# First feed-forward block as plain products, raw chunks of both weights in one tile, pools on 64 bytes

## The chip, the cores and the metric

The kernel runs on one core of one Trainium2 chip. The metric is device time in microseconds (us), the median of several runs of the whole program; lower is better. All times below are us, unless ns is written. PE is TensorE, DVE is VectorE, ACT is ScalarE, SP is SyncE, which issues the weight loads.

## The reference

One decoder layer on a residual stream x of 256 rows and 2,048 columns, in fp32: two half-weight SwiGLU feed-forwards around a mixer (gated linear attention beside block attention) and a cross-attention.

```python
D_MODEL = 2048; SEQ = 256; D_FF = 5632

def swiglu(h, w_gate, w_up, w_down):
    return (jax.nn.silu(h @ w_gate) * (h @ w_up)) @ w_down

x = x + 0.5 * swiglu(rms_norm(x, ffn1_norm[l]), ffn1_w_gate[l], ffn1_w_up[l], ffn1_w_down[l])
u = rms_norm(x, mix_norm[l]) @ w_in[l]      # split into the inputs of the two head groups
x = x + jnp.concatenate([o_gla, o_moba], axis=-1) @ w_out[l]
x = x + memory_cross_attn(rms_norm(x, xattn_norm[l]), rms_norm(mem, mem_norm[l]), ...)
x = x + 0.5 * swiglu(rms_norm(x, ffn2_norm[l]), ffn2_w_gate[l], ffn2_w_up[l], ffn2_w_down[l])
```

## The kernel before

**Products.** Each fp32 product is made of three products of rounded halves (`mm3`): high by high, high by low, low by high, 512 columns wide, into one PSUM bank. A weight comes raw from memory in chunks of 128 rows by 512 columns, two chunks in one load of 512 KB (`load_raw`, issued by SP, tag `raw`, five buffers). ACT writes its high half (`whi`, L142), DVE subtracts that from the raw one for the low half (`wlo`, L143); both tags have five buffers of two chunks (three in the mixer).

**Feed-forward (`ffn`).** The 5,632 hidden columns are 11 blocks of 512, in groups of 4, 4 and 3. For a block, `Pair` makes gate and up for both halves of the rows together, on seven of the eight PSUM banks, in eight steps of two chunks of 128 of the 2,048 input rows. In its first four steps (S) it forms sums of raw gate and up chunks (tag `st`, four DVE operations of 512, L217 to L220), splits four things (the gate's two chunks, the up's second chunk u1 as `hu`/`lu`, and the two tiles of sums) and makes seven threefold products, against rows of x and prepared sums of them (`eh`/`el`). The last four steps (N) split gate and up plainly and make eight threefold products, against x and its differences (`dh`/`dl`). That is 84 + 96 = 180 products for a pair; plain gate and up would take 192. `early`, `gates` and `ups` then combine the banks on DVE (seven operations of 512), and L422 multiplies gate and up. `turn` transposes the result for the down product while the next pair runs; `pump` puts such pieces of work behind each step. After a group, four down blocks use its 16 (or 12) chunks. `run_blocks(late=True)` leaves the last four chunks of the first two blocks for behind the remaining work of `turn` (`drain`).

**Norm (`Normed`).** x is normed in four blocks of 512 columns: PE transposes four tiles of 128 (L315) into the one auxiliary bank, DVE scales them (`xg`, L318, with a broadcast gain), ACT and DVE split them (`xhi`, `xlo`), and for the pairs the sums of x for S steps (L364, and `eh`/`el`) or its differences for N steps (L369, and `dh`/`dl`) follow. In both feed-forwards this goes on while the first pair's products run.

**Order.** Each engine runs its instructions in one order, set before the program runs by the framework's scheduler, which also takes the waits for buffers from the pools. So lines of code and places in an engine's order differ, as the listings below show.

## Time and profile before

| | |
|---|---|
| median of three runs | 2019.07 (2018.95 to 2019.37) |
| profiled execution | 2019.1, its span 2017.4 |
| mean granted PE clock | 0.994 of full |
| PE busy | 1966.3 (97%) |
| DVE busy | 1531.9 (76%) |
| ACT busy | 1061.7 (53%) |
| weights moved | 369 MB, 183 GB/s in the mean |
| first pair of feed-forward 1, of 2 | 13.8 to 81.6, 1273.6 to 1335.4 |

A busy time is the time in which an engine executes something. Of an average over a span that has stages with different limits one learns little; the rows below are therefore taken by stretch. A start-to-start time of two neighbours is what an operation costs a busy engine; the recorded duration of one is longer, since neighbours overlap. In a row with square brackets the engine was idle for the time in them, up to the operation named.

### The profile page before, as it was taken

The page shows a single profiled execution, that of the slowest core. Times are in us where ns is not written, and L with a number is a line of the kernel's source. Part 1 is how long each engine was busy: PE and PEld are TensorE (multiplying, and loading weights), DVE is VectorE, ACT ScalarE, POOL GpSimd, SP SyncE. Part 2 cuts the span into 40 slices and gives each one's busy share as a digit, 9 for nine tenths or more (in the row PEclk, how much of TensorE's full clock was granted, in tenths as well). Part 3 has the DMA queues.
Part 4 walks back from the last instruction along what each step waited for, and adds up shares of the span by engine and source line. Part 5 has one row for each costly group of instructions (what it writes and reads, how often), then busy time and mean ns, then how long its engine had stood idle before and what let it go on. Part 6 is the DMA issues. An engine that isn't in the chain of part 4 may idle for free.

```text
span 2017.4 us, 24213 instructions
## 1 busy us (share of the span) xinstructions
PE 1966.3 (97%) x8848; PEld 1588.0 (79%) x8848; DVE 1531.9 (76%) x1974; ACT 1061.7 (53%) x1326; POOL 23.5 (1%) x52
## 2 busy tenths in 40 slices
PE   6999999999999999999999999899999999999999
PEld 4777888778887788887788888677788777888777
DVE  7998569996599865455765767999856999569974
ACT  5655445564455545544564646655544565445542
POOL 0000000000000000010000000000000000000000
PEclk8999999999999999999999999899999999999999
DMA  4566665556665656565456545366655556655564
GB/s 157 187 191 207 200 190 173 187 188 219 194 193 187 198 161 187 154 201 159 142 168 204 171 158 186 95 197 210 196 189 170 186 191 199 213 188 188 177 220 136
DMA packets 195487, 369.19 MB, mean 183 GB/s; under 512 B 11716, under 2 KB 22168, under 8 KB 195368
## 3 DMA queue, kind: packets, MB, share of 16 engines
q1 hardware_dynamic: 195368, 367.65, 57.6%
q8 instruction: 69, 1.13, 0.2%
q14 instruction: 50, 0.41, 0.1%
HBM read 365.50 MB, written 2.10 MB: 182 GB/s over the span
## 4 chain that ended last, share of the span: by engine, by line
PE 77%; DVE 16%; ACT 2%; issue 2%; DMA 2%; ACTq 0%; SPq 0%; DVEq 0%
PE mm L154 25%; PE mm L155 25%; PE mm L156 24%; DVE wlo L143 7%; ACT whi L142 2%; DVE st L217 1%; DMA raw<-in_ffn_w_up_dram 1%; DVE st L218 1%; DVE t2k L422 1%; DVE st L219 1%; DVE st L220 1%; DVE lu L143 1%; PE aux L315 1%; DVE biglo L143 0%; DVE xlo L143 0%
## 5 line engine op out<-in xcount | busy, mean ns | idle before, releaser
L143 DVE TENSOR_TENSOR wlo<-raw,whi 128x1024 fp32r<-128x1024 f32 (+3 forms) x616 | 732.6, 1200 | 389.6 <-ACT whi L142 388.8
L142 ACT ACTIVATE whi<-raw 128x1024 fp32r<-128x1024 f32 (+3 forms) x616 | 630.0, 1037 | 616.9 <-PE mm L156 510.4
L155 PE MATMUL mm<-wlo,xhi 128*128 128x512 f32 (+2 forms) x1240 | 485.0, 391 | 3.7 <-DVE wlo L143 3.7
L154 PE MATMUL mm<-whi,xhi 128*128 128x512 f32 (+2 forms) x1240 | 482.7, 393 | 1.0 <-ACT whi L142 1.0
L156 PE MATMUL mm<-whi,xlo 128*128 128x512 f32 (+2 forms) x1240 | 480.2, 387 | 0.0
L156 PE MATMUL mm<-whi,biglo 128*128 128x512 f32 x864 | 338.5, 392 | 0.0
L154 PE MATMUL mm<-whi,bighi 128*128 128x512 f32 x832 | 329.9, 396 | 0.0
L155 PE MATMUL mm<-wlo,bighi 128*128 128x512 f32 x832 | 323.9, 389 | 0.0
L155 PEld LDWEIGHTS mm<-wlo,xhi 128*128 128x128 f32 x1240 | 234.4, 189 | 53.1 <-DVE wlo L143 10.5
L154 PEld LDWEIGHTS mm<-whi,xhi 128*128 128x128 f32 x1240 | 234.0, 189 | 48.8 <-ACT whi L142 2.1
L156 PEld LDWEIGHTS mm<-whi,xlo 128*128 128x128 f32 x1240 | 234.3, 189 | 47.1
L142 ACT ACTIVATE whi<-st 128x1024 fp32r<-128x1024 f32 x176 | 185.8, 1059 | 130.2 <-DVE st L218 59.2
L143 DVE TENSOR_TENSOR wlo<-st,whi 128x1024 fp32r<-128x1024 f32 x176 | 212.6, 1220 | 6.2 <-ACT whi L142 5.0
L156 PEld LDWEIGHTS mm<-whi,biglo 128*128 128x128 f32 x864 | 162.2, 188 | 37.6
L155 PEld LDWEIGHTS mm<-wlo,bighi 128*128 128x128 f32 x832 | 156.3, 188 | 33.3
L154 PEld LDWEIGHTS mm<-whi,bighi 128*128 128x128 f32 x832 | 156.5, 188 | 30.9
L154 PE MATMUL mm<-whi,eh 128*128 128x512 f32 x264 | 106.1, 417 | 18.9 <-ACT whi L142 16.5
L155 PE MATMUL mm<-wlo,eh 128*128 128x512 f32 x264 | 106.8, 405 | 2.5 <-DVE wlo L143 1.0
L156 PE MATMUL mm<-whi,el 128*128 128x512 f32 x264 | 103.4, 392 | 0.0
L142 ACT ACTIVATE hu<-raw 128x512 fp32r<-128x512 f32 x88 | 55.4, 630 | 87.7 <-DMA raw<-in_ffn_w_up_dram 59.7
L154 PEld LDWEIGHTS mm<-whi,eh 128*128 128x128 f32 x264 | 49.3, 193 | 45.1 <-ACT whi L142 36.6
L217 DVE TENSOR_TENSOR st<-raw,raw 128x512 f32<-128x512 f32 x88 | 60.6, 688 | 23.7 <-DMA raw<-in_ffn_w_up_dram 22.9
(211 smaller groups left out, 1833.6 us busy)
## 6 DMA issues: line engine op xcount, KB each, us to landing
raw<-in_ffn_w_gate_dram SPq DMA_DIRECT2D x176, 512.0 KB, 4.6
raw<-in_ffn_w_up_dram SPq DMA_DIRECT2D x176, 512.0 KB, 3.9
raw<-in_ffn_w_down_dram SPq DMA_DIRECT2D x176, 512.0 KB, 4.1
raw<-in_w_in_dram SPq DMA_DIRECT2D x80, 512.0 KB, 3.9
raw<-in_w_out_dram SPq DMA_DIRECT2D x32, 512.0 KB, 3.6
raw<-in_w_in_dram SPq DMA_DIRECT2D x16, 344.0 KB, 3.1
raw<-in_xattn_w_kv_dram SPq DMA_DIRECT2D x8, 512.0 KB, 3.6
raw<-in_xattn_w_q_dram SPq DMA_DIRECT2D x8, 512.0 KB, 3.5
```

Of the source, the lines that this page charges most:

```text
L142: nc.scalar.activation(hi, src, AF.Copy)
L143: nc.vector.tensor_tensor(lo, src, hi.bitcast(F32), op=ALU.subtract)
L154: nc.tensor.matmul(p, a[0], w[0], start=start, stop=False)
L155: nc.tensor.matmul(p, a[0], w[1], start=False, stop=False)
L156: nc.tensor.matmul(p, a[1], w[0], start=False, stop=stop)
L217: nc.vector.tensor_tensor(sa[:, 0, :], g[:, 0, :], u[:, 0, :], op=ALU.add)
L218: nc.vector.tensor_tensor(sa[:, 1, :], u[:, 0, :], u[:, 1, :], op=ALU.add)
L219: nc.vector.tensor_tensor(sb[:, 0, :], sa[:, 0, :], u[:, 1, :], op=ALU.add)
L220: nc.vector.tensor_tensor(sb[:, 1, :], sb[:, 0, :], g[:, 1, :], op=ALU.add)
L315: nc.tensor.transpose(pt[:, i, :], c[:, i * P:(i + 1) * P], ident)
L422: nc.vector.scalar_tensor_tensor(u, u, r, g, op0=ALU.mult, op1=ALU.mult)
```

## The change

The lines of the kernel after are other ones: the sums are at L232, L234 and L235, `split_to` at L153 (DVE), the products at L165 to L167, the transposes of the norm at L328, the scaling at L331.

- The first block of each feed-forward is a plain gate block and a plain up block, two banks each, through `run_blocks(late=True)`. `gate_done` takes silu from PSUM on ACT, `up_done` multiplies on DVE. The other ten blocks stay pairs.
- A raw tile holds four chunks; there are three. A plain block loads four chunks in one DMA (1 MB). A pair's step loads gate into slots 1 and 2 and up into slots 0 and 3 of one tile, so the two sums (gate's first + up's first, up's first + up's second) are one DVE operation of 1,024 with a broadcast operand.
- `whi` and `wlo` have six buffers, and u1 takes one of these; `hu` and `lu` go.
- Ahead of the norm only the first four gate chunks are loaded.
- The two tiles of gains get a size that is a multiple of 64 bytes, by which all pools behind them start at such a multiple (before: 32 bytes off). In the mixer two small constants share the tile of `mqT`, which is made later.

```diff
@@ -43,8 +43,8 @@
 OFF_MQ = OFF_LR + RANK
 OFF_MK = OFF_MQ + BH * DH
 OFF_MV = OFF_MK + BH * DH
-RAWS = 5
-HIS = 5
+RAWS = 3
+HIS = 6
 T2K = 7
 KINDS = "SSSSNNNN"
 
@@ -94,8 +94,8 @@
     nc.scalar.activation(warm, warm, AF.Silu)
     ident = const.tile([P, P], F32, name="ident")
     make_identity(nc, ident)
-    gT1 = const.tile([P, KC], F32, name="gT1")
-    gT2 = const.tile([P, 4 * KC + 4], F32, name="gT2")
+    gT1 = const.tile([P, 32], F32, name="gT1")[:, :KC]
+    gT2 = const.tile([P, 96], F32, name="gT2")[:, :4 * KC + 4]
     gT = [gT1] + [gT2[:, i * KC:(i + 1) * KC] for i in range(4)]
     g_mq, g_mk, g_xq, g_xk = (gT2[:, 4 * KC + i:4 * KC + i + 1] for i in range(4))
 
@@ -128,26 +128,37 @@
 
     ahead = {}
 
-    def load_raw(k0, c0, w, n=NB):
-
-        raw = wp.tile([P, 2, n], F32, tag="raw", name=nm("raw"))
-        nc.sync.dma_start(raw, w[k0 * P:(k0 + 2) * P, c0:c0 + n].rearrange("(k p) n -> p k n", p=P))
+    def raw_tile():
+        return wp.tile([P, 4, NB], F32, tag="raw", name=nm("raw"))
+
+    def load_raw(k0, c0, w, n=NB, step=4):
+
+        raw = raw_tile()[:, :step, :n]
+        nc.sync.dma_start(raw, w[k0 * P:(k0 + step) * P, c0:c0 + n].rearrange("(k p) n -> p k n", p=P))
         return raw
 
-    def take_raw(k0, c0, w, n=NB):
+    def take_raw(k0, c0, w, n=NB, step=4):
         key = id(w), k0, c0
-        return ahead.pop(key) if key in ahead else load_raw(k0, c0, w, n)
+        return ahead.pop(key) if key in ahead else load_raw(k0, c0, w, n, step)
+
+    def load_pair(k0, c0, wg, wu):
+
+        raw = raw_tile()
+        for dst, w in ((raw[:, 1:3, :], wg), (raw[:, 0:4:3, :], wu)):
+            nc.sync.dma_start(dst, w[k0 * P:(k0 + 2) * P, c0:c0 + NB].rearrange("(k p) n -> p k n", p=P))
+        return raw
 
     def split_to(hi, lo, src):
         nc.scalar.activation(hi, src, AF.Copy)
         nc.vector.tensor_tensor(lo, src, hi.bitcast(F32), op=ALU.subtract)
 
-    def split_raw(raw, n=NB):
-
+    def split_raw(raw):
+
+        k, n = raw.shape[1:]
         bufs = 3 if "mix" in pools else HIS
-        hi, lo = (tmp_tile([P, 2, n], tag, bufs, F32R) for tag in ("whi", "wlo"))
+        hi, lo = (tmp_tile([P, 2, NB], tag, bufs, F32R)[:, :k, :n] for tag in ("whi", "wlo"))
         split_to(hi, lo, raw)
-        return [(hi[:, i, :], lo[:, i, :]) for i in range(2)]
+        return [(hi[:, i, :], lo[:, i, :]) for i in range(k)]
 
     def mm3(p, a, w, start, stop):
 
@@ -168,13 +179,17 @@
 
         def step(self, k0, nk=4):
             hi, lo = self.a
-            for k2 in range(k0, k0 + nk, 2):
-                ws = split_raw(take_raw(self.w_k0 + k2, self.c0, self.w, self.n), self.n)
-                for t in range(NT):
-                    s = slice(t * P, (t + 1) * P)
-                    for i, w in enumerate(ws):
-                        k = k2 + i
-                        mm3(self.ps[t], (hi[:, k, s], lo[:, k, s]), w, k == 0, k == self.nk - 1)
+            k2 = k0
+            while k2 < k0 + nk:
+                raw = take_raw(self.w_k0 + k2, self.c0, self.w, self.n, min(4, k0 + nk - k2))
+                for i in range(0, raw.shape[1], 2):
+                    ws = split_raw(raw[:, i:i + 2])
+                    for t in range(NT):
+                        s = slice(t * P, (t + 1) * P)
+                        for k, w in enumerate(ws, k2 + i):
+                            mm3(self.ps[t], (hi[:, k, s], lo[:, k, s]), w, k == 0,
+                                k == self.nk - 1)
+                k2 += raw.shape[1]
             pump()
             if k0 + nk == self.nk:
                 self.done(self.ps)
@@ -204,27 +219,25 @@
             if self.begun is None:
                 self.begun = set()
             a = self.a
-            g = take_raw(2 * q, self.c0, self.wg)
-            u = take_raw(2 * q, self.c0, self.wu)
+            raw = load_pair(2 * q, self.c0, self.wg, self.wu)
+            g, u2 = raw[:, 1:3], raw[:, 3:4]
             if KINDS[q] == "N":
-                gs, us = split_raw(g), split_raw(u)
+                gs, us = split_raw(g), split_raw(raw[:, 0:4:3])
                 for name, t, ws in (("p2", 0, gs), ("q4", 1, gs), ("r3", None, us), ("r5", 1, us)):
                     for i, w in enumerate(ws):
                         x = a.diff(2 * q + i) if t is None else a.plain(t, 2 * q + i)
                         self.add(name, x, w, i == 1)
             else:
                 sa, sb = (tmp_tile([P, 2, NB], "st") for _ in range(2))
-                nc.vector.tensor_tensor(sa[:, 0, :], g[:, 0, :], u[:, 0, :], op=ALU.add)
-                nc.vector.tensor_tensor(sa[:, 1, :], u[:, 0, :], u[:, 1, :], op=ALU.add)
-                nc.vector.tensor_tensor(sb[:, 0, :], sa[:, 0, :], u[:, 1, :], op=ALU.add)
-                nc.vector.tensor_tensor(sb[:, 1, :], sb[:, 0, :], g[:, 1, :], op=ALU.add)
-                hu, lu = (tmp_tile([P, NB], tag, 2, F32R) for tag in ("hu", "lu"))
-                gs = split_raw(g)
-                split_to(hu, lu, u[:, 1, :])
+                nc.vector.tensor_tensor(sa, raw[:, 1:4:2], raw[:, 0:1].to_broadcast([P, 2, NB]),
+                                        op=ALU.add)
+                nc.vector.tensor_tensor(sb[:, 0:1], sa[:, 0:1], u2, op=ALU.add)
+                nc.vector.tensor_tensor(sb[:, 1, :], sb[:, 0, :], raw[:, 2, :], op=ALU.add)
+                gs, (us,) = split_raw(g), split_raw(u2)
                 sums = split_raw(sa) + split_raw(sb)
                 e, o = 2 * q, 2 * q + 1
                 for name, x, w in (("p1", a.plain(0, e), gs[0]), ("p2", a.plain(0, o), gs[1]),
-                                   ("r3", a.comb(3, q), (hu, lu)),
+                                   ("r3", a.comb(3, q), us),
                                    ("r5", a.comb(0, q), sums[0]), ("r7", a.comb(2, q), sums[1]),
                                    ("r6", a.comb(1, q), sums[2]), ("q4", a.plain(1, o), sums[3])):
                     self.add(name, x, w, True)
@@ -407,11 +420,25 @@
                         yield
                 yield
 
-            for b in range(b0, b1):
+            sg = {}
+
+            def gate_done(ps):
+                for t in range(NT):
+                    sg[t] = half_kb()
+                    nc.scalar.activation(sg[t], ps[t], AF.Silu, scale=a.rstd[:, t:t + 1])
+
+            def up_done(ps):
+                h = [half_kb() for _ in range(NT)]
+                for t in range(NT):
+                    nc.vector.scalar_tensor_tensor(h[t], ps[t], a.rstd[:, t:t + 1], sg[t],
+                                                   op0=ALU.mult, op1=ALU.mult)
+                behind.append(turn(0, h))
+
+            if b0 == 0:
+                run_blocks([(a, wg, 0, KC, gate_done), (a, wu, 0, KC, up_done)], late=True)
+            for b in range(max(b0, 1), b1):
                 pair = Pair(a, wg, wu, b * NB)
                 for q in range(KC // 2):
-                    if b == 0 and q == KC // 2 - 2:
-                        drain()
                     pair.step(q)
                     if q == KINDS.rindex("S"):
                         pair.early()
@@ -456,13 +483,9 @@
             n1.block(j)
             yield
 
-    def load_ahead(k0):
-        for w in (w1g, w1u):
-            ahead[id(w), k0, 0] = load_raw(k0, 0, w)
-
-    load_ahead(0)
+    ahead[id(w1g), 0, 0] = load_raw(0, 0, w1g, step=2)
     load_x(1)
-    load_ahead(2)
+    ahead[id(w1g), 2, 0] = load_raw(2, 0, w1g, step=2)
     load_x(2)
     load_x(3)
     n1.block(0)
@@ -512,11 +535,12 @@
     nc.gpsimd.memset(mask[:CH, 0:1], 1.0 / TAU)
     nc.gpsimd.memset(mask[CH:, 1:2], 1.0 / TAU)
     nc.gpsimd.tensor_copy(m_ch, mask)
-    bg = pools["own"].tile([P, GQK], F32, name="bg")
+    early = own_tile([P, BH, T], "s8d")
+    bg = early[:, 0:2].rearrange("p a b -> p (a b)")
     nc.sync.dma_start(bg, gla_b_gate2.to_broadcast([P, GQK]))
     go = pools["own"].tile([P, GDV], F32, name="go")
     nc.sync.dma_start(go, gla_out_norm.to_broadcast([P, GDV]))
-    wg2 = pools["own"].tile([RANK, GQK], F32, name="wg2")
+    wg2 = early[:RANK, 2:4].rearrange("p a b -> p (a b)")
     nc.sync.dma_start(wg2, gla_w_gate2[0])
 
     oh = act_tile([P, KC, T], "bighi", F32R)
...
```

DVE at the start of the program, before. `raw_96` and `raw_98` are the first loads of gate and up, `xg`, `xhi`, `xlo` those of the norm's first block, `aux` its transposes:

```order
L143 TENSOR_TENSOR wlo_213<-raw_96,whi_212 128x1024
L106 COPY gT_79<-aux_93 128x16
L217 TENSOR_TENSOR st_204<-raw_96,raw_98 128x512
L218 TENSOR_TENSOR st_204<-raw_98 128x512
L318 TENSOR_TENSOR xg_119<-aux_114,gT_79 128x512
L219 TENSOR_TENSOR st_205<-st_204,raw_98 128x512
L143 TENSOR_TENSOR lu_211<-raw_98,hu_210 128x512
L143 TENSOR_TENSOR xlo_108<-xg_119,xhi_107 128x4x128
L318 TENSOR_TENSOR xg_130<-aux_125,gT_79 128x512
L220 TENSOR_TENSOR st_205<-st_205,raw_96 128x512
L364 TENSOR_TENSOR xg_136<-xg_130 128x128
```

And after, where `raw_96` and `raw_99` both belong to the gate, and L377 is the norm's sums for the later pairs:

```order
L153 TENSOR_TENSOR wlo_198<-raw_96,whi_197 128x1024
L106 COPY gT_79<-aux_93 128x16
L331 TENSOR_TENSOR xg_115<-aux_110,gT_79 128x512
L153 TENSOR_TENSOR wlo_214<-raw_99,whi_213 128x1024
L153 TENSOR_TENSOR xlo_104<-xg_115,xhi_103 128x4x128
L331 TENSOR_TENSOR xg_126<-aux_121,gT_79 128x512
L377 TENSOR_TENSOR xg_132<-xg_126 128x128
L377 TENSOR_TENSOR xg_132<-xg_126,xg_115 128x128
L377 TENSOR_TENSOR xg_132<-xg_115,xg_132 128x128 x2
L153 TENSOR_TENSOR xlo_104<-xg_126,xhi_103 128x4x128
```

The four sums of raw chunks, the split of u1 and the splits of sums have left the start; the second gate split and the norm's own work stand there now.

DVE in the second S step of a pair, with a piece of `turn` (`biglo`) in it; before, that of block 1:

```order
L217 TENSOR_TENSOR st_739<-raw_735,raw_737 128x512
L218 TENSOR_TENSOR st_739<-raw_737 128x512
L219 TENSOR_TENSOR st_740<-st_739,raw_737 128x512
L143 TENSOR_TENSOR wlo_748<-raw_735,whi_747 128x1024
L220 TENSOR_TENSOR st_740<-st_740,raw_735 128x512
L143 TENSOR_TENSOR lu_746<-raw_737,hu_745 128x512
L143 TENSOR_TENSOR wlo_754<-st_739,whi_753 128x1024
L143 TENSOR_TENSOR biglo_196<-aux_728,bighi_195 128x4x128
L143 TENSOR_TENSOR wlo_758<-st_740,whi_757 128x1024
```

After, that of block 2:

```order
L232 TENSOR_TENSOR st_1022<-raw_1019 128x1024
L153 TENSOR_TENSOR wlo_1028<-raw_1019,whi_1027 128x1024
L234 TENSOR_TENSOR st_1023<-st_1022,raw_1019 128x512
L153 TENSOR_TENSOR wlo_1032<-raw_1019,whi_1031 128x512
L235 TENSOR_TENSOR st_1023<-st_1023,raw_1019 128x512
L153 TENSOR_TENSOR biglo_192<-aux_1012,bighi_191 128x4x128
L153 TENSOR_TENSOR wlo_1036<-st_1022,whi_1035 128x1024
L153 TENSOR_TENSOR wlo_1040<-st_1023,whi_1039 128x1024
```

Of the four sums in a row three operations are left, with a split of the gate between the first and the second, and the split of u1 is a `wlo`.

PE at the start of feed-forward 1, before. `mm_197` to `mm_203` are the seven banks of the pair, `whi_285` the split of the second gate load:

```order
L154 MATMUL mm_197<-whi_212,xhi_107 128x512
L155 MATMUL mm_197<-wlo_213,xhi_107 128x512
L154 MATMUL mm_200<-whi_212,xhi_107 128x512
L155 MATMUL mm_200<-wlo_213,xhi_107 128x512
L156 MATMUL mm_197<-whi_212,xlo_108 128x512
L156 MATMUL mm_200<-whi_212,xlo_108 128x512
L315 MATMUL aux_150<-ident,x_sb 128x128 x4
L154 MATMUL mm_197<-whi_285,xhi_107 128x512
L154 MATMUL mm_200<-whi_285,xhi_107 128x512
L154 MATMUL mm_202<-hu_210,eh_110 128x512
L155 MATMUL mm_202<-lu_211,eh_110 128x512
```

After, where `mm_193` and `mm_194` are the gate's two banks and `whi_213` the second gate load's split:

```order
L165 MATMUL mm_193<-whi_197,xhi_103 128x512
L166 MATMUL mm_193<-wlo_198,xhi_103 128x512
L167 MATMUL mm_193<-whi_197,xlo_104 128x512
L165 MATMUL mm_193<-whi_197,xhi_103 128x512
L166 MATMUL mm_193<-wlo_198,xhi_103 128x512
L328 MATMUL aux_146<-ident,x_sb 128x128 x4
L167 MATMUL mm_193<-whi_197,xlo_104 128x512
L165 MATMUL mm_193<-whi_213,xhi_103 128x512
L165 MATMUL mm_194<-whi_197,xhi_103 128x512
L166 MATMUL mm_194<-wlo_198,xhi_103 128x512
L166 MATMUL mm_193<-wlo_214,xhi_103 128x512
```

Where products of one split went to several banks with rows of x and with sums of x, twelve products of one split now go to two banks with rows of x alone; the transposes of the next norm block stand after the fifth of them, where they stood after the sixth.

## Rows read from the trace of the kernel before

**Rows 1.** The page's busy tenths of the span in 40 slices.

```profile
PE   6999999999999999999999999899999999999999
...
DVE  7998569996599865455765767999856999569974
```

**Rows 2.** Stretches: us, busy time (instructions) of each engine, clock, DMA share, GB/s.

```profile
13.81:82.90 69.09, 60.14 (x228) 45.80 (x226) 66.13 (x111) 44.24 (x62) 0.00 (x0) 0.90 0.50 160
1273.60:1336.70 63.10, 54.48 (x218) 41.00 (x216) 60.56 (x95) 37.47 (x49) 0.00 (x0) 0.92 0.49 155
...
126.50:170.70 44.20, 43.35 (x188) 33.76 (x187) 41.99 (x52) 25.31 (x29) 0.00 (x0) 1.00 0.58 191
213.50:300.00 86.50, 86.50 (x383) 71.02 (x382) 51.40 (x53) 35.15 (x35) 0.00 (x0) 1.00 0.59 187
...
22.00:28.70 6.70, 3.81 (x22) 2.97 (x20) 6.41 (x14) 4.96 (x8) 0.00 (x0) 1.00 0.09 34
39.60:50.00 10.40, 9.67 (x26) 6.92 (x26) 10.19 (x22) 4.18 (x8) 0.00 (x0) 0.54 0.36 102
```

**Rows 3.** Timeline of PE: start, duration, line, tiles; full clock, then half.

```profile
777.25 0.39 PE L154 MATMUL mm<-whi,xhi 128*128 128x512 f32 x1
...
779.31 0.39 PE L154 MATMUL mm<-whi,xhi 128*128 128x512 f32 x1
...
29.28 0.63 PE L155 MATMUL mm<-wlo,xhi 128*128 128x512 f32 x1
...
31.41 0.63 PE L155 MATMUL mm<-lu,eh 128*128 128x512 f32 x1
```

**Rows 4.** The chain that ended last: start, duration, what, in order of time.

```profile
1118.44 0.87 PE aux L315 x8
```

**Rows 5.** Timelines of PE and DVE: first product and close of both first pairs.

```profile
13.81 0.80 PE L154 MATMUL mm<-whi,xhi 128*128 128x512 f32 x1
...
81.56 1.41 DVE L422 SCALAR_TENSOR_TENSOR t2k<-t2k,r,t2k 128x512 f32<-128x512 f32 x2
...
1273.60 0.39 PE L154 MATMUL mm<-whi,xhi 128*128 128x512 f32 x1
...
1335.38 1.41 DVE L422 SCALAR_TENSOR_TENSOR t2k<-t2k,r,t2k 128x512 f32<-128x512 f32 x2
```

**Rows 6.** Timeline of PE in the first pair: idle time before, and its releaser.

```profile
28.69 0.80 PE L154 MATMUL mm<-whi,eh 128*128 128x512 f32 x1 [2.89 <-ACT whi L142]
...
39.58 1.12 PE L315 MATMUL aux<-ident,x_sb 128*128 128x128 f32 x4 [2.97 <-DVE xg L318]
```

**Rows 7.** Timeline of DVE in an S step of a later pair.

```profile
130.80 0.69 DVE L218 TENSOR_TENSOR st<-raw 128x512 f32<-128x512 f32 x1
131.40 0.69 DVE L219 TENSOR_TENSOR st<-st,raw 128x512 f32<-128x512 f32 x1
132.00 1.23 DVE L143 TENSOR_TENSOR wlo<-raw,whi 128x1024 fp32r<-128x1024 f32 x1
133.14 0.69 DVE L220 TENSOR_TENSOR st<-st,raw 128x512 f32<-128x512 f32 x1
```

**Rows 8.** Groups of DVE by line and form: count, busy, mean ns, idle before.

```profile
L318 DVE TENSOR_TENSOR xg<-aux,gT 128x512 f32<-128x512 f32 x40 | 26.9, 686 | 7.1 <-PE aux L315 7.1
...
L364 DVE TENSOR_TENSOR xg<-xg,xg 128x128 f32<-128x128 f32 x24 | 6.1, 285 | 0.0
```

**Rows 9.** Waits of DVE in 344 to 390: us in total, times, longest.

```profile
DVE st L217 <- DMA raw<-in_ffn_w_up_dram: 1.9, 1, 1.9
DVE wlo L143 <- ACT whi L142: 1.9, 2, 1.4
```

**Rows 10.** Timeline of PE: first products of threes in a block of 344 columns.

```profile
828.33 0.31 PE L154 MATMUL mm<-whi,xhi 128*128 128x344 f32 x1
...
828.79 0.32 PE L154 MATMUL mm<-whi,xhi 128*128 128x344 f32 x1
...
829.27 0.31 PE L154 MATMUL mm<-whi,xhi 128*128 128x344 f32 x1
```

More of the change, by code (lines that the diff above doesn't have):

```diff
@@ L526, in hymba_layer @@
     qkT = own_tile([P, 2, GH, T], "s8c")
-    mqT = own_tile([P, BH, T], "s8d")
     ktail = own_tile([P, NT, GQK], "s4a")
@@ L755, in moba_scores @@
             psx = aux_tile([P, 3 * P])
-            nc.tensor.matmul(psx[:, :P], mqT[:, h, :P], mixer["mkT"][:, h, :P], start=True,
+            nc.tensor.matmul(psx[:, :P], mixer["mqT"][:, h, :P], mixer["mkT"][:, h, :P], start=True,
                              stop=True)
-            nc.tensor.matmul(psx[:, P:], mqT[:, h, P:], mixer["mkT"][:, h, :], start=True,
+            nc.tensor.matmul(psx[:, P:], mixer["mqT"][:, h, P:], mixer["mkT"][:, h, :], start=True,
                              stop=True)
@@ L792, in mq_done, with f @@
     def mq_done(j):
-        return lambda ps: head_norm(ps, n2.rstd, g_mq, mqT[:, 4 * j:4 * j + 4, :])
+        def f(ps):
+            if j == 0:
+                mixer["mqT"] = own_tile([P, BH, T], "s8d")
+            head_norm(ps, n2.rstd, g_mq, mixer["mqT"][:, 4 * j:4 * j + 4, :])
+        return f
     def mk_done(j):
```

## The prediction

> **What bounds the kernel now.** I read the busy tenths of the span first [rows 1]: TensorE (PE) stands at 9 in nearly every slice, with a 6 in the first and an 8 some two thirds in. Those two places are the starts of the two feed-forwards, and there and in the rest of each feed-forward VectorE (DVE) is near 9 too. The table of stretches says which engine limits where [rows 2]. In the first pair of feed-forward 1 (13.81 to 82.90) DVE is busy 66.1 us of 69.1 and PE 60.1, with the clock at 0.90; in that of feed-forward 2, DVE 60.6 of 63.1 and PE 54.5. A later pair (126.5 to 170.7) is nearly balanced, with PE 43.4 and DVE 42.0 of 44.2. A group of down blocks is PE alone: 86.50 of 86.50, DVE 51.4.
>
> PE's floor is its cadence. Nine products of 512 columns after 777.25 the next starts at 779.31, so 0.229 us each; at the clock's lower level (1.2 GHz) five take from 29.28 to 31.41, 0.426 each [rows 3]. A pair has 180 such products, 41.2 us; with two quads of transposes at 0.44 (eight take 0.87 [rows 4]) 42.1. A later pair so stands 2.1 us over its floor, and the first pairs, from their first product to the operation that closes them (the product of gate and up, L422; 13.81 to 81.56, and 1273.60 to 1335.38 [rows 5]), 67.75 and 61.78 us, that is 26 and 20 us over 41.2.
>
> What fills that excess stands in the gaps [rows 6]: PE idles 2.89 us before 28.69 for a split, and 2.97 before 39.58 for a scaled block of the norm; after each the clock falls. In 22.00 to 28.70 the clock is full, DVE is busy 6.41 of 6.70 and PE 3.81; in 39.60 to 50.00 the granted clock is 0.54 and PE's busy 9.67 us are spent at half speed [rows 2]. So the first pairs are limited by DVE, which makes norm, sums and splits at once, and pay for its lateness a second time in the clock.
>
> **The first block in plain products.** Plain gate and up blocks take 2 x 16 x 2 x 3 = 192 products where the pair took 180: 12 x 0.229 = 2.7 us more of PE for each feed-forward. What DVE loses in that block: the sums of four S steps (4 x 4 operations whose next start comes 0.60 later [rows 7]: 9.6 us), the splits of sums (4 x 2 x 1.14 = 9.1) and of u1 (the up weight's second chunk, 4 x 0.60 = 2.4), and some seven operations of combining (4.2); it gains the full splits of up in the S steps, 4 x 1.14 = 4.6. So 20.7 us less, and 66.1 becomes 45.4, 60.6 becomes 39.9. The norm's own work stays, since later pairs need its sums and differences. After: PE 44.0 plus six quads of transposes and the gains (2.8), DVE 45.4; both near 46, where one had 66.
>
> Feed-forward 1 then adds up so: 44.0 + 2.8, + 4.1 for the low clock at the start (full from about 22.0, 8.2 us at half speed; the start at 13.81 I leave where it is), + 1.0 from the last product to the closing operation, + stalls. For these the floor is none, and the other end is one gap like those shown with its stretch at half clock: 2.9, and some six products at 0.426 instead of 0.229 behind it [rows 3] another 1.2, together 4.1. I take 3.5, near the upper end, since DVE must still make three of the four norm blocks inside the gate's products. Sum 55.4 against 67.75: **-12.3**. Feed-forward 2: 44.0 + 4 quads (1.8) + 1.0 + 3.0 = 49.8 against 61.78: **-12.0**. Without any gap the two are 6.5 better together, with one gap each 1.7 worse.
>
> **Two sums in one operation.** In the 20 pairs that stay, each of four S steps replaces two sums of 512 by one of 1,024. Starts are 0.60 apart after a 512 operation and 1.14 after a 1,024 one [rows 7], so 0.06 is saved each: 80 x 0.065 = **-5.2**. That the one sum has a broadcast operand costs nothing by the nearest row: the norm's scaling with a broadcast operand runs 686 ns for 512 [rows 8], as the plain sums do. It counts in full only where DVE sets the pace; in a balanced pair half may be hidden, so -2.6 to -5.2.
>
> Here the page "VectorE: DVE Perf Modes" of the Trainium skill, section "The DRAIN you can't avoid", speaks of a larger gain: an operation is followed by a flush, and the next does not start until the pipe is empty. By it two operations of 0.69 would cost 1.38 against 1.23, and 80 x 0.15 = 12 us would be saved, the sum -39, the time 1980. The rows disagree: the next operation starts 0.09 before the record of the one before it ends; the page itself adds that an operation that is not held starts earlier.
>
> **Loads and buffers.** Raw chunks go from five buffers of two chunks to three of four; in a pair the lead goes from 2.5 steps to 3. The splits go from five to six buffers, but u1 now takes one of them: in an S step 5/3 of a step of lead becomes 6/4, in an N step 5/2 becomes 3. DVE waits in a sample pair 1.9 us for an up load and 1.9 us for ScalarE's splits [rows 9], both around the turn from N steps to S steps. The wait for the load can shrink, the one for the split can grow. Bounds: the whole excess of the pairs over PE's floor gone, 20 x 2.1 = -42, or a new wait of the same size in every pair, +38. Taken: **-2**, since the lead changes by half a step either way. SyncE issues a third of its loads less; the downs are all PE [rows 2], and one load of 1 MB serves 5.5 us of products there, so nothing is taken off or added. The shared tile in the mixer moves no operation of length: 0, with 2 us either way.
>
> **Pools on 64 bytes.** Nothing is taken for it. In the blocks of 344 columns a tile's second chunk starts 32 bytes off from the first (344 x 4 = 1,376 bytes, 21.5 times 64), so both alignments alternate there: triples start at 828.33, 828.79 and 829.27 [rows 10]. One takes 0.46, the other 0.48; no large effect, and of unclear sign.
>
> The page "VectorE: DVE Perf Modes", section "The TRN2 errata — SBUF-src ops pay a fixed extra latency per instruction", of the Trainium skill gives 215 ns for a product of 512 columns. The trace has 229 [rows 3]; if start addresses were the reason for the difference, its figure would take off 7,900 x 14 = 110 us, and the time would be near 1880 (rival C).
>
> **Sum.** The profiled execution took 2019.1 us, 2017.4 of them its span; the median of the runs is 2019.07, so they are one. -12.3 - 12.0 - 5.2 - 2 = -31.5: 1987.6, taken as **1987**.
>
> **Rivals.**
> B: the starts gain little. The gate's first 48 products (11 us at full clock) need two more norm blocks, which the pair spread over 30 us; ahead of these DVE's order has six splits (6.8), five scalings and eight further operations of 512 (7.8) and sixteen small sums (285 ns each in the record [rows 8], 0.2 from start to start: 3.2), some 18 us. PE would idle and run at half clock again: gains of 0 to 12 at the starts, with 5 to 7 in the pairs: 2000 to 2014. For it: the row at 39.58, a PE that waits for a scaled block [rows 6]. Against: DVE's total of 45 fits PE's 47, the sums for later pairs can wait, and up's products, which need only what is already normed, stand ready.
> C: the 64-byte starts speed up every product. At the full clock of 2.4 GHz 512 columns are 213 ns, and rows show 229; half of the 16 ns on some 7,900 products is -62, so 1925. Against: in the 344-column rows PE's cadence is the same on either alignment to within 0.02 per triple [rows 10].
> D: the 64-byte starts slow them. If the longer triple there is that of the whole-line starts, 0.01 to 0.02 per triple of 2,630 is +26 to +53: 2014 to 2041. It makes the kernel slower from 0.014 per triple on.
> E: u1 in the shared buffers. Per pair one wait more of 1.9 us for a split, as in the rows 9, at the turn to the S steps: 20 x 1.9 = +38, so 2026, and slower than before from 1.8 us per pair on. Against: DVE reached the sample's waits twice in 46 us only, and the N steps ahead of the turn get more buffers.
> F: the change moves what it says, but the time stays: the scheduler puts the norm's sums for later pairs so early that the first block keeps its 67 us: 2012 to 2019.
>
> **How the numbers follow.** Chances: forecast 0.66 (1974 to 2003: starts without a gap and some more off the pairs, to half of the starts' gain lost), B 0.12, C 0.09, D 0.04, E 0.05, F 0.04. A measurement tells about 0.2%, 4 us, from no change. Faster: A, B and C, 0.87. Same: F and an edge of D, 0.05. Slower: E and the rest of D, 0.08. The range runs from 1966 (starts without a gap, -30.8, and half of the pairs' excess, -21) to 2014 (B's end); outside lie most of C, D and E, 0.2.
>
> **What would show it.** Right: from first product to the closing operation about 55 us in feed-forward 1 and 50 in feed-forward 2, with the clock full from the 25th us on and DVE still above 0.9; later pairs near 43.8 from close to close; the 1,024 sum followed by the next start 1.14 later; down groups at 86.5 as before. Wrong: a cadence of 512 columns away from 0.229 (C, D); pairs above 44.2 with PE waiting for a split of sums or of u1 (E); gaps of 3 us before scaled norm blocks in the gate's products (B).

## The result, and the profile after

The median is 1985.95 us (1984.32 to 1988.44, four runs) against 2019.01 (2017.67 to 2019.37, four runs) beside it: 0.9839 of before, with a 95% interval of 0.9821 to 0.9856. The profiled execution took 1984.34, its span 1982.6. The predicted time was 1987.

In PE's busy tenths of the page of after, beside [rows 1], the first slice went from 6 to 7, and the 8 of feed-forward 2's start is gone.

The table of stretches (columns as in [rows 2]) for the two first blocks:

```profile
11.73:63.50 51.77, 50.18 (x221) 39.77 (x220) 46.19 (x78) 33.28 (x48) 0.00 (x0) 1.00 0.68 224
1255.34:1301.50 46.16, 46.05 (x209) 37.62 (x208) 39.05 (x62) 26.33 (x36) 0.00 (x0) 1.00 0.60 200
```

The first blocks went from 69.1 and 63.1 us to 51.8 and 46.2; DVE's work in them fell from 66.1 and 60.6 to 46.2 and 39.1. The down groups stayed: from the close of a group's last pair to the first product of the next pair, 86.80 in both kernels.

Laid end to end from the timelines (the product of gate and up closes a block: L433 of the plain one, L449 of a pair), the spans differ so:

| stretch | before | after | difference | predicted |
|---|---|---|---|---|
| start to first product | 13.81 | 11.73 | -2.1 | 0 |
| feed-forward 1, first product to close of the first block | 67.75 | 51.11 | -16.6 | -12.3 |
| its ten later pairs and down blocks | 682.4 | 681.1 | -1.3 | -3.6 |
| mixer and cross-attention, to feed-forward 2's first product | 509.6 | 511.4 | +1.8 | 0 |
| feed-forward 2, first product to close of the first block | 61.78 | 45.45 | -16.3 | -12.0 |
| its ten later pairs and down blocks | 678.3 | 677.9 | -0.4 | -3.6 |
| end | 3.7 | 4.0 | +0.2 | 0 |
| sum | | | -34.7 | -31.5 |

So almost all of the gain lies in the two first blocks, more than forecast, and the later pairs gave 1.7 where 7.2 was forecast. (The profiled execution gains 34.7, the medians 33.1.) That small sum hides two movements. Of the 20 pairs, counted from close to close, two follow a plain block, four follow a group of down blocks, six are the last of a group, and the other eight are called middle pairs here. The middle pairs took 44.2 to 46.0 before and 43.9 to 44.0 now (-7.7 together). The last pairs of the six groups went from 43.03 to 43.6 (+3.7), the first pairs behind a down group from 43.05 or 43.24 to 43.4 (+1.3), those behind the plain block from 44.5 to 45.0 (+1.0). The experiments part these.

### The profile page after: what moved, and what is told of

It is laid out like the page before. It is cut to its first block, busy times and chain, and to the rows that moved or that the text cites. A ratio compares the mean times of both kernels' runs of the same rounds, so it can differ in the third digit from the quotient of the medians.

```text
span 1982.6 us, 23399 instructions
## 1 busy us (share of the span) xinstructions
PE 1945.7 (98%) x8872; PEld 1590.8 (80%) x8872; DVE 1489.4 (75%) x1832; ACT 1047.5 (53%) x1308; POOL 23.5 (1%) x52
## 3 DMA queue, kind: packets, MB, share of 16 engines
q8 instruction: 69, 1.13, 0.2%
## 4 chain that ended last, share of the span: by engine, by line
PE 77%; DVE 17%; ACT 3%; issue 2%; DMA 1%; SPq 0%; ACTq 0%
PE mm L165 24%; PE mm L167 24%; PE mm L166 24%; DVE wlo L153 8%; ACT whi L152 3%; DVE st L232 2%; DVE st L235 2%; DVE st L234 1%; DVE biglo L153 1%; DVE t2k L449 1%; PE aux L328 1%; DVE t2k L256 0%; DVE t2k L265 0%; DVE t2k L269 0%; DVE t2k L259 0%
## 5 line engine op out<-in xcount | busy, mean ns | idle before, releaser
L153 DVE TENSOR_TENSOR wlo<-raw,whi 128x1024 fp32r<-128x1024 f32 (+3 forms) x704 | 796.3, 1142 | 377.1 <-ACT whi L152 375.1
L152 ACT ACTIVATE whi<-raw 128x1024 fp32r<-128x1024 f32 (+3 forms) x704 | 683.5, 989 | 661.6 <-PE mm L167 561.1
L165 PE MATMUL mm<-whi,xhi 128*128 128x512 f32 (+2 forms) x1296 | 507.7, 392 | 1.0 <-ACT whi L152 1.0
L167 PE MATMUL mm<-whi,xlo 128*128 128x512 f32 (+2 forms) x1296 | 500.9, 387 | 0.0
L167 PE MATMUL mm<-whi,biglo 128*128 128x512 f32 x864 | 338.8, 392 | 0.1
L165 PE MATMUL mm<-whi,bighi 128*128 128x512 f32 x832 | 329.6, 396 | 0.0
L167 PEld LDWEIGHTS mm<-whi,xlo 128*128 128x128 f32 x1296 | 243.7, 188 | 51.3 <-DVE xlo L153 1.1
L165 PEld LDWEIGHTS mm<-whi,xhi 128*128 128x128 f32 x1296 | 243.7, 188 | 50.9 <-ACT whi L152 1.9
L152 ACT ACTIVATE whi<-st 128x1024 fp32r<-128x1024 f32 x160 | 167.5, 1059 | 168.5 <-PE mm L167 78.9
L153 DVE TENSOR_TENSOR wlo<-st,whi 128x1024 fp32r<-128x1024 f32 x160 | 192.7, 1222 | 43.7 <-ACT whi L152 42.2
L167 PEld LDWEIGHTS mm<-whi,biglo 128*128 128x128 f32 x864 | 162.1, 188 | 37.7 <-DVE biglo L153 0.6
L165 PEld LDWEIGHTS mm<-whi,bighi 128*128 128x128 f32 x832 | 156.4, 188 | 31.2
L165 PE MATMUL mm<-whi,eh 128*128 128x512 f32 x320 | 122.7, 400 | 17.5 <-ACT whi L152 17.5
L166 PE MATMUL mm<-wlo,eh 128*128 128x512 f32 x320 | 125.5, 392 | 0.2
L167 PE MATMUL mm<-whi,el 128*128 128x512 f32 x320 | 125.1, 391 | 0.0
L232 DVE TENSOR_TENSOR st<-raw 128x1024 f32<-128x1024 f32 x80 | 97.6, 1220 | 1.2 <-DMA raw<-in_ffn_w_up_dram 0.5
L165 PEld LDWEIGHTS mm<-whi,eh 128*128 128x128 f32 x320 | 60.0, 188 | 41.9 <-ACT whi L152 30.0
L166 PEld LDWEIGHTS mm<-wlo,eh 128*128 128x128 f32 x320 | 60.1, 188 | 14.3 <-DVE wlo L153 1.9
```

The source lines that it names most:

```text
L152: nc.scalar.activation(hi, src, AF.Copy)
L153: nc.vector.tensor_tensor(lo, src, hi.bitcast(F32), op=ALU.subtract)
L165: nc.tensor.matmul(p, a[0], w[0], start=start, stop=False)
L166: nc.tensor.matmul(p, a[0], w[1], start=False, stop=False)
L167: nc.tensor.matmul(p, a[1], w[0], start=False, stop=stop)
L232: nc.vector.tensor_tensor(sa, raw[:, 1:4:2], raw[:, 0:1].to_broadcast([P, 2, NB]), op=ALU.add)
```

## The experiments

Theory after the comparison: the first block in plain products brings the whole gain, because it takes DVE's work off the place where DVE was late; of the rest, something gives in the pairs and something takes away. The rival is the prediction's own sum: 24 from the first blocks, 7 from the pairs.

Behind "Measured" stand the median, its ratio to the kernel before run beside it (2017.6 to 2018.6), and the 95% interval of that ratio. The fifth, sixth and eleventh experiment have two runs each, the second nine, the others four. They are numbered in the order in which they were set up; the ninth stands ahead of the seventh here, the twelfth ahead of the eleventh. In the diffs `...` marks code left out.

**One part alone, and the rest alone.** Into the kernel before, the plain first block and the loads ahead of it:

```diff
...
+            if b0 == 0:
+                run_blocks([(a, wg, 0, KC, gate_done), (a, wu, 0, KC, up_done)], late=True)
-            for b in range(b0, b1):
+            for b in range(max(b0, 1), b1):
...
-        for w in (w1g, w1u):
-            ahead[id(w), k0, 0] = load_raw(k0, 0, w)
+        ahead[id(w1g), k0, 0] = load_raw(k0, 0, w1g)
```

> The kernel before with one part of the change: the first block of each feed-forward plain on four banks, and the gate chunks alone loaded ahead. Theory: the whole gain is in the two first blocks and the earlier start, so about 33 to 35 us come off, 1984 to 1987; first product near 11.7, first block closed near 63 in feed-forward 1, and 45 to 46 us from first product to close in feed-forward 2. Rival (the terms of the prediction): the starts bring 24 us, 1995, and the rest of the gain is in the pairs.

Measured: 1986.43, 0.9845 (0.983 to 0.9859); first product at 13.16, feed-forward 1's first block 50.8 from there, feed-forward 2's 45.2. The part alone gives what the whole change gives, without the earlier start that the theory counted in (13.16 instead of 11.7). The rest alone, from the kernel after:

```diff
-            if b0 == 0:
-                run_blocks([(a, wg, 0, KC, gate_done), (a, wu, 0, KC, up_done)], late=True)
-            for b in range(max(b0, 1), b1):
+            for b in range(b0, b1):
...
-    ahead[id(w1g), 0, 0] = load_raw(0, 0, w1g, step=2)
+    ahead[id(w1g), 0, 0] = load_pair(0, 0, w1g, w1u)
...
```

> The kernel after without that part: a pair again as first block, its first two steps loaded ahead; one operation for two sums, raw ring, six split buffers and 64 bytes stay. Theory: the pairs together give 1 to 3 us, 2016 to 2018, with middle pairs at 44.0 (before 44.2 to 46.0) and the last pair of a group at 43.7 (before 43.0). Rival (the prediction's terms): -7, 2012.

Measured: 2013.71, 0.9978 (0.9968 to 0.9988): 4.3 us (2.4 to 6.5 by the interval), between theory and rival. Middle pairs 43.9, last ones 43.6. Its first pair took 67.2 us from first product (11.76) to close, 67.75 before: merging and buffers do next to nothing for a block that DVE's norm holds up.

**The 64 bytes.** The two gain tiles at their old sizes:

```diff
-    gT1 = const.tile([P, 32], F32, name="gT1")[:, :KC]
-    gT2 = const.tile([P, 96], F32, name="gT2")[:, :4 * KC + 4]
+    gT1 = const.tile([P, KC], F32, name="gT1")
+    gT2 = const.tile([P, 4 * KC + 4], F32, name="gT2")
```

> The kernel after with the two gain tiles at their old size, so that the pools start 32 bytes off a multiple of 64 again, nothing else. Theory: no difference, 1984 to 1988, 512 columns at 0.229 us each. Rivals: aligned starts speed products up (this one is slower, by 4 us for each half ns on a product) or slow them (faster by as much).

Measured: 1985.71, 0.984 (0.9825 to 0.9855), down groups 87.14 in both. Starts on 64 bytes do nothing here (the median from start to start of two products is 229 ns with and without); rivals C and D are out.

**The merged sums.** Two operations again:

```diff
-                nc.vector.tensor_tensor(sa, raw[:, 1:4:2], raw[:, 0:1].to_broadcast([P, 2, NB]),
-                                        op=ALU.add)
+                for i in range(2):
+                    nc.vector.tensor_tensor(sa[:, i], raw[:, 1 + 2 * i], raw[:, 0], op=ALU.add)
```

> The kernel after with the two sums of sa as two operations of 512 again, nothing else. The scheduler then puts L234 right behind them and the split of u1 behind L235. Theory: the merged operation gives nothing, since it lets the split of u1 in ahead of the second tile of sums; 1981 to 1986, last pairs of a group back from 43.7 to 43.0 to 43.2. Rival (the prediction's term): DVE sets the pace, 80 x 0.065 = 5 us slower, 1990 to 1993.

Measured: 1985.14, 0.9839 (0.9822 to 0.9855). The merged sums give nothing, as theory said; but its reason for the longer last pairs fell, since these stay at 43.6 to 43.7 with L234 right behind the sums and u1 behind L235. So the next pair of runs asked for u1's buffers.

**u1's buffers.** Kernel after, u1 in its own two buffers, and the other side, the first experiment's kernel with u1 in the shared ones:

```diff
-HIS = 6
+HIS = 5
...
-                gs, (us,) = split_raw(g), split_raw(u2)
+                us = tuple(tmp_tile([P, NB], tag, 2, F32R) for tag in ("hu", "lu"))
+                gs = split_raw(g)
+                split_to(*us, raw[:, 3, :])
```

> The kernel after with the split of u1 in two buffers of its own again (and five instead of six buffers for the other splits); the raw tiles of four chunks and the one operation for two sums stay. It asks why a group's last pair takes 43.66 after and 43.03 before. Theory U (u1 takes a whole split buffer, so that splits run less far ahead): last pairs back at 43.0 to 43.1. Theory R (the raw tile holds gate and up until the later of them is used): still 43.6 to 43.7.

Measured: 1977.38, 0.9794 (0.9775 to 0.9814); last pairs 42.9 to 43.0, middle ones 43.2 to 43.4.

```diff
-HIS = 5
+HIS = 6
...
-                hu, lu = (tmp_tile([P, NB], tag, 2, F32R) for tag in ("hu", "lu"))
+                hu, lu = (tmp_tile([P, 2, NB], tag, HIS, F32R)[:, 0, :] for tag in ("whi", "wlo"))
```

> The other side: the kernel of the first experiment (plain first block, else as before) with u1 in one of six shared split buffers; raw loads of two chunks and four sums of 512 stay. Theory U: last pairs 43.6 to 43.7. Theory R: they stay at 43.0. In both, the middle pairs stay at 44.4 to 45.2 if the loads of two chunks cause these.

Measured: 1986.25, 0.9838 (0.9819 to 0.9858); last pairs 43.6. Both say theory U for the last pairs. Where the 0.6 us sit is seen in PE's timeline of a group's last pair, its rows with idle time: first the kernel after (two gaps), then u1 in its own buffers (one):

```profile
166.15 0.50 PE L165 MATMUL mm<-whi,eh 128*128 128x512 f32 x1 [0.45 <-ACT whi L152]
...
169.07 0.50 PE L165 MATMUL mm<-whi,eh 128*128 128x512 f32 x1 [0.80 <-ACT whi L152]
```

```profile
169.49 0.50 PE L165 MATMUL mm<-whi,eh 128*128 128x512 f32 x1 [0.82 <-ACT whi L152]
```

The first gap is the loss: the product at 166.15 starts 0.84 us behind the one before it, where the cadence is 0.23. It stands 14.3 us behind the pair's opening (151.86), in the third of the four S steps, which fits a lead of the splits that S steps in a row use up. With loads of two chunks (the sixth experiment) the middle pairs got shorter by the shared buffers, 43.9 to 44.3 but for one of 46.4, against 44.4 to 45.2, as the last ones got longer; there the time stays as it is (1986.25 against 1986.43).

**What gives in the pairs.** The edits of the fourth and the fifth experiment together, u1 in its own buffers and the sums apart:

```diff
...
+                for i in range(2):
+                    nc.vector.tensor_tensor(sa[:, i], raw[:, 1 + 2 * i], raw[:, 0], op=ALU.add)
...
+                us = tuple(tmp_tile([P, NB], tag, 2, F32R) for tag in ("hu", "lu"))
...
```

> The kernel after with u1 in two buffers of its own and the two sums as two operations again; of the change in the pairs only the raw tiles of four chunks are left. It parts the gain of the fifth experiment (pairs at 43.0 to 43.3, 1977). If the merged operation gives it, this one is 5 us slower, 1981 to 1984, pairs 0.2 to 0.3 longer. If the raw tiles give it, it stays at 1976 to 1979, and the waits for loads that made some middle pairs of before 45 to 46 are gone in both.

Measured: 1977.36, 0.9796 (0.9781 to 0.981), the same as with merged sums. So the raw tiles of four chunks give it: against the first experiment's kernel 9 us less, middle pairs 43.4 to 43.8 where they were 44.4 to 45.2. From 328 to 372.5 ACT waits 7.6 us for loads in the first experiment's profile and 2.5 in this one. The new tiles also hold twelve chunks where the old ones held ten; the size of a tile and the room of the ring were not tried apart. And the 9 us come only with u1 in its own buffers: from the sixth experiment's kernel (1986.25) to the fourth's (1985.14), both with u1 in the shared ones, the same tiles give 1.

Why merging gives nothing shows in the timelines of DVE and ACT in the last S step of a last pair; first merged, u1 in its own buffers:

```profile
164.13 1.22 DVE L232 TENSOR_TENSOR st<-raw 128x1024 f32<-128x1024 f32 x1
...
167.60 0.69 DVE L235 TENSOR_TENSOR st<-st,raw 128x512 f32<-128x512 f32 x1
...
168.38 1.06 ACT L152 ACTIVATE whi<-st 128x1024 fp32r<-128x1024 f32 x1 [0.23 <-DVE st L235]
```

and with the sums apart:

```profile
163.43 1.29 DVE L233 TENSOR_TENSOR st<-raw 128x512 f32<-128x512 f32 x2
...
166.37 0.68 DVE L235 TENSOR_TENSOR st<-st,raw 128x512 f32<-128x512 f32 x1
...
167.27 0.60 ACT L251 ACTIVATE t2k<-mm 128x512 f32<-128x512 f32 x1 [1.41 <-PE mm L167]
167.77 1.05 ACT L152 ACTIVATE whi<-st 128x1024 fp32r<-128x1024 f32 x1
```

The merged operation takes 1.13 from start to start (the next, a split, starts at 165.26) instead of 1.20, as forecast. But what PE waits for is the split of the second tile of sums. That tile is ready 4.16 us behind the first sum's start when merged (164.13 to 168.29) and 3.62 apart (163.43 to 167.05), since two splits now stand between the three operations. Merged, ACT waits for the tile (0.23). Apart, the tile waits 0.72 for ACT, which first copies a bank whose last product PE makes late (L251). The product that uses the split starts at 169.49 and 168.87, 16.63 and 16.72 us behind the pair's opening (152.86, 152.15): the same place. So what is saved on DVE does not reach PE in either order. PE's idle time before that product, 0.82 and 0.43, is no measure of it; apart, smaller delays stand ahead of it.

**The order of the steps.** If four S steps in a row are what holds a pair up, S and N steps in turn should free it:

```diff
-KINDS = "SSSSNNNN"
+KINDS = "SNSNSNSN"
```

> The kernel after with the steps of a pair in the order S N S N S N S N instead of S S S S N N N N; the work is the same. Theory: the 1.5 to 2 us that a pair takes over PE's floor come from four S steps in a row, in which DVE needs 6.4 to 7.0 us a step and PE 4.8; in turn with N steps (DVE 2.3, PE 5.5) a lead of one step covers it, so pairs come to 42.3 to 43.0 and the time to 1955 to 1970. Rival: the three banks that S steps alone fill are now read off at the end of the pair instead of its middle, together with the five other combinations, and the next pair's first products wait for these banks: pairs at 44 to 45, 1985 to 2005.

Measured: 1955.22, 0.9687 (0.967 to 0.9703), 31 us less than the kernel after and 63 less than before, the fastest kernel of this study. A middle pair in the table of stretches:

```profile
108.62:150.61 41.99, 41.99 (x189) 34.58 (x189) 41.73 (x49) 25.59 (x30) 0.00 (x0) 1.00 0.59 201
```

PE is busy all of it, near the prediction's floor of 42.1, and DVE 41.73 of 41.99: in turn, the two just fit.

```diff
-KINDS = "SSSSNNNN"
+KINDS = "SSNSNSNN"
```

> The same with S S N S N S N N: two N steps stay behind the last S step, which give time to read off the three banks. Theory: the same 42.3 to 43.0 or a little more from the two S steps at the start; 1955 to 1975. If the rival of the run before holds, this one lies well below that run; if pairs are bounded by something other than the S steps' DVE work, both stay at 1984 to 1988.

Measured: 1957.83, 0.9698 (0.9683 to 0.9712), not told apart from the run before by the intervals. Last pairs are shorter (41.4 to 41.7 against 41.5 to 42.4), pairs behind the plain block longer (45.0 to 45.3 against 44.2 to 44.3). The rival, that reading the banks off late costs, isn't seen.

The kernel of the fifth experiment with the order in turn:

```diff
-KINDS = "SSSSNNNN"
+KINDS = "SNSNSNSN"
```

> Steps in the order S N S N S N S N and u1 in its own two buffers. If u1's place costs as much with this order, 1945 to 1949; if the order has already taken DVE off the path, as theory says (pairs at 41.5 to 42.7, near PE's floor of 42.1), no more than 2 us either way, 1953 to 1957.

Measured: 1957.29, 0.9694 (0.9678 to 0.971), 2 us more than with shared buffers, with intervals that overlap. u1's place, worth 8.6 with S steps in a row, is worth nothing that shows once the order has taken S steps apart; pairs behind a down group are 43.7 to 43.9 against 42.7 here, last ones 40.8 to 41.2 against 41.5 to 42.4. The kernel of the first experiment with the same edit:

> The kernel of the first experiment (plain first block, else as before: loads of two chunks, four sums of 512, u1 in its own buffers) with the steps in the order S N S N S N S N. It asks whether the raw tiles of four chunks, the merged sums and the six split buffers do anything once DVE has room between S steps. Theory: no, 1955 to 1960, pairs at 41.5 to 43. Rival: the loads of two chunks hold the pairs up whatever the order, as in the middle pairs of before at 45 to 46; 1970 to 1980.

Measured: 1972.81, 0.9778 (0.9762 to 0.9795). The time lies in the rival's range, but not for the rival's reason: middle and last pairs are at 41.2 to 43.4, near what theory has. Instead the first pairs behind a down group take 45.5 to 47.5, and the down groups 87.5 to 89.8 (to DVE's last operation on them; 87.14 in the kernels before and after). One of these, near 581, in the timelines of ACT and of PE:

```profile
580.85 0.63 ACT L142 ACTIVATE hu<-raw 128x512 fp32r<-128x512 f32 x1 [5.41 <-DMA raw<-in_ffn_w_up_dram]
581.39 0.71 ACT L435 ACTIVATE t2k<-t2k,r 128x512 f32<-128x512 f32 x1
```

```profile
586.25 0.77 PE L154 MATMUL mm<-whi,eh 128*128 128x512 f32 x1 [4.27 <-DVE t2k L256]
586.81 0.63 PE L155 MATMUL mm<-wlo,eh 128*128 128x512 f32 x1
```

ACT waits 5.41 us for an up load of the next pair, with the silu of the pair that ends standing behind it; the banks come free late, PE idles 4.27, and the products behind that are recorded with 0.63 instead of 0.39, as at the clock's lower level in [rows 3]. Between this kernel and the tenth experiment's lie 15.5 us; they differ by the raw tiles, the merged sums and the 64 bytes, of which the last two gave nothing elsewhere. So the raw tiles are worth some 15 us in this order, against 9 with S steps in a row; the intervals leave it open whether that is more. That ACT's order, silu behind that split, costs this was read from the timeline and not tried by itself. The order in turn is thus worth 31 us in the kernel after, 20 with u1 in its own buffers, and 14 with loads of two chunks.

**The start.** Two loads more at the places of before's first up loads:

```diff
     ahead[id(w1g), 0, 0] = load_raw(0, 0, w1g, step=2)
+    spare = act_tile([P, KC, T], "bighi")
+    nc.sync.dma_start(spare[:, 0:4, :].rearrange(...), w1u[0:2 * P, :NB].rearrange(...))
     load_x(1)
     ahead[id(w1g), 2, 0] = load_raw(2, 0, w1g, step=2)
+    nc.sync.dma_start(spare[:, 4:8, :].rearrange(...), w1u[2 * P:4 * P, :NB].rearrange(...))
```

> The kernel after with two more loads of 512 KB (of the up weight, into a tile that is not in use yet, and not read there) at the places where the kernel before had its first two loads of up. Theory: the first block of x then lands later again, as before; the first scaled norm block and the first product slip by about 2 us, from 11.7 to 13.5 to 13.9, and the time rises by about 2, 1987 to 1990. Rival: the first product came earlier since DVE has no sums of raw chunks to make ahead of it; then it stays at 11.7 to 12.0.

Measured: 1990.11, 0.9858 (0.9838 to 0.9877). First product at 13.00, but the profiles of the other experiments with a plain first block, without these loads, stand at 12.8 to 13.4 too; only the kernel after's has 11.73, and the second experiment, with both up loads ahead, 11.76. Neither theory nor rival explains this. The first block of x is not late: ACT reads it at 4.8 to 5.2 in all fourteen profiles. PE's first transposes of it wait for something else, as in the kernel after:

```profile
6.61 1.06 ACT L152 ACTIVATE whi<-raw 128x1024 fp32r<-128x1024 f32 x1 [0.30 <-DMA raw<-in_ffn_w_gate_dram]
...
9.06 1.11 PE L328 MATMUL aux<-ident,x_sb 128*128 128x128 f32 x4 [3.69 <-DVE gT L106]
```

The transposed gains stand in the one auxiliary bank until DVE copies them (L106), and in DVE's order that copy stands behind the low half of the first gate load, which waits for ACT's split. That split starts between 6.35 (second experiment) and 8.55 us (before), and the first product follows 5.1 to 5.4 behind it in every profile. So it is the first gate load whose landing differs by up to 2 us between the profiles; why was not found, and copying the gains first was not tried.

The time of this kernel, 4 us more, is not clear of the kernel after's by the intervals. Its profile shows where the loads can cost. The first block closes at 69.1 instead of 62.8 to 65.4, with a gap in PE's timeline, a low clock behind it (table of stretches), and the cause in ACT's:

```profile
26.37 0.80 PE L165 MATMUL mm<-whi,xhi 128*128 128x512 f32 x1 [3.08 <-ACT whi L152]
```

```profile
24.00:30.00 6.00, 3.10 (x8) 2.00 (x9) 5.97 (x17) 4.87 (x7) 0.00 (x0) 0.55 0.31 115
```

```profile
24.74 0.63 ACT L152 ACTIVATE eh<-xg 128x512 fp32r<-128x512 f32 x1 [1.50 <-DVE xg L377]
```

ACT makes the split that PE waits for at 25.28, behind a split of the norm's sums for later pairs, for which DVE is late. In the kernel after the same two stand the other way round, the weight's split at 20.92 and that of the sums at 22.81.

## Why the prediction was right, point by point

The mechanism was right for the first blocks, where the gain is. That the total came out 1 us from the forecast is in part luck: the first blocks gave 8.6 more than forecast and the pairs 5.5 less.

- **What bounds the kernel**: right. DVE's load in the first blocks was forecast at 45.4 and 39.9 and measured 46.2 and 39.1, and with it went the gaps of [rows 6] and the stretches at half clock behind them. One sign was missed: DVE's busy share of the two blocks is 0.89 and 0.85, not above 0.9.
- **First blocks, -24.3**: right in mechanism, too small in size, -32.9. The terms that were mis-sized are the stalls, 3.5 and 3.0, the low clock at the start, 4.1, and the 1.0 from the last product to the closing operation, in both. In feed-forward 1 PE's timeline has two gaps:

```profile
22.01 0.73 PE L165 MATMUL mm<-whi,xhi 128*128 128x512 f32 x2 [0.95 <-ACT whi L152]
23.27 0.50 PE L166 MATMUL mm<-wlo,xhi 128*128 128x512 f32 x1 [0.53 <-DVE wlo L153]
```

  1.5 us of idle time (2.0 by the starts, beyond the cadence), and no low clock behind them; in feed-forward 2 no idle time is recorded. The clock is up by 16, where it took until 22: products start 0.43 apart at 13.55 and 0.23 apart from 15.56 on:

```profile
13.55 0.63 PE L165 MATMUL mm<-whi,xhi 128*128 128x512 f32 x1
13.98 0.63 PE L166 MATMUL mm<-wlo,xhi 128*128 128x512 f32 x1
...
15.56 0.62 PE L165 MATMUL mm<-whi,xhi 128*128 128x512 f32 x2
16.02 0.63 PE L166 MATMUL mm<-wlo,xhi 128*128 128x512 f32 x2
```

  From 11.73 to 15.56 PE makes six products and four transposes and loses 2.1 us against its full cadence, instead of 4.1. The closing operation costs nothing behind the products, since it takes the first half of the rows while PE still works on the second: in feed-forward 2 it starts when 191 of the block's 192 products have started.

```profile
1300.79 1.40 DVE L433 SCALAR_TENSOR_TENSOR t2k<-mm,r,t2k 128x512 f32<-128x512 f32 x2
```

  Rival B stood for the gap that did not come. The eleventh experiment's profile shows that it can come, with its low clock, when ACT's order puts the norm's sums ahead of a weight's split. The stall was taken near its upper end, though DVE's total fitted PE's.
- **Merged sums, -5.2**: wrong, 0 in both kernels where it was taken out. The step that failed is "It counts in full only where DVE sets the pace", by which the term was taken in full: DVE's operation got shorter by what the rows said, but PE waits for a split of one of its results, and that split ends at the same place either way, held by DVE's later tile in one order and by ACT in the other. The flush that the Trainium skill ("VectorE: DVE Perf Modes", "The DRAIN you can't avoid") gives, and with it a gain of 12 us, is not seen either: the operation behind the merged one starts 1.13 later, that behind two plain ones 1.20.
- **Loads and buffers, -2**: right as a sum, and by luck: the two parts are not small, and they do not add. Taken in one order, the raw tiles give -9 (first against ninth experiment) and u1 in the shared buffers +8.6 (fifth against the kernel after); taken in the other, u1 changes nothing (sixth) and the raw tiles give -1 (fourth). The statement that the lead changes by half a step either way had both signs, but not their size. Rival E's mechanism is real, at 0.4 us a pair in the mean (8.6 over 20), not 1.9, and in the third S step, not at the turn from N to S. (SyncE issues 515 weight loads instead of 704, so a quarter less and not a third; nothing was taken for it.)
- **64 bytes, 0**: right. The 215 ns that the Trainium skill states for a product of 512 columns ("VectorE: DVE Perf Modes", "The TRN2 errata — SBUF-src ops pay a fixed extra latency per instruction") are not reached on either alignment: PE's products stay 0.23 apart.
- **Start and mixer, 0 each**: -2.1 and +1.8 in the profiled runs. Of the first, most is the run's own (above). Of the second, 0.4 is one quad of transposes more that now stands ahead of feed-forward 2's first product (five, before four), and 0.8 one gap in the cross-attention's output, near 1236.9: ACT's split there stands behind splits of a weight that wait for their loads (three waits, 6.3 us in all). The rest was not found. The stretch takes 510.0 to 510.5 in the three other kernels that load two chunks at a time (first, sixth, twelfth), and 511.0 to 512.1 with four chunks.

## What to carry to other kernels

Where two engines share a stage, compare the order of their heavy and light steps before counting instructions: taking turns was worth 31 us, without one instruction fewer (14 to 20 in kernels with other buffers). Judge a merged operation by when the product that waits for its result can start, not by the engine's sum. Before a small buffer is merged into a shared pool, ask how far each user of the pool may then run ahead. Try such parts on more than one base: the raw tiles were worth 9 us in one kernel and 1 in another.

## What the runs showed of the hardware that was not expected

The first gate load, 512 KB and issued at 1.81 in the kernels before and after, was first used by ACT between 6.35 and 8.55 us, with no relation to the loads behind it in these runs. From the first product on, PE went over to its full cadence near 15.6 in the kernel after and only near 22 in the kernel before, from starts 2 us apart; in the kernel before PE had idled 0.97 us ahead of 18.56. What decides it was not tried. In the stretch where products of the kernel after are 0.43 apart the table of stretches shows the granted clock at 1.00, and so it does from 13.8 to 21.7 in the kernel before; at the start of these profiles the intervals, not that column, tell the level:

```profile
11.73:15.60 3.87, 3.84 (x13) 2.68 (x12) 3.63 (x10) 3.80 (x10) 0.00 (x0) 1.00 0.30 72
```
